# Low halves of the token mix's weights: from a VectorE subtraction to an accumulating transfer

## The chip, the cores and the metric

The kernel runs on one core of one Trainium2 chip. The metric is the device time of one execution in microseconds (us), shown as a median over several runs. Beside it stands one profiled execution with its own time; its trace is where every duration below comes from.

The core has five engines with instruction queues of their own, each worked off in order. PE (TensorE) multiplies matrices; DVE (VectorE), ACT (ScalarE) and POOL (GpSimd) work element by element; SP (SyncE) issues transfers here. Engines wait for one another by semaphores. Transfers (DMA) are carried out by 16 DMA engines that all queues share.

## The reference, cut to what matters

One layer of a decoder with 512 prompt tokens and 64 sample tokens (576 columns), width 1024. A SwiGLU feed-forward stage, then the token mix, then a second feed-forward stage.

```python
z = h @ w_in                                   # 1024 x 10240
u, v, q, k, rv, rg, ga, gb = split(z)
o_a = gelu(u) * chunk_spatial_mix(layer_norm(gelu(v)), gm_ws, gm_bs)
o_r, S_new = retention(rotary(q), rotary(k), rv, S0)        # 8 heads
o_b = head_rms(o_r) * silu(rg)
merged = sigmoid(ga) * (o_a @ w_a) + sigmoid(gb) * (o_b @ w_b)
x = x + g2 * (merged @ w_o)
```

All is float32. The kernel gets its accuracy by splitting each operand into a high part (rounded to the format fp32r) and a low part (the rest, also fp32r), and adds three products: high by high, high by low and low by high.

## The kernel before, in words

Activations lie with features on the 128 partitions and the 576 tokens along the row. A weight matrix is taken in pieces of 128 x 1024 elements (512 KB): eight row blocks of 128 columns, or four blocks of 256, or two of 512.

A piece of the token mix goes through three steps. `load_raw` issues its transfer from HBM on SP's queue into a buffer `wraw`; in the token mix there are three of these. `split_w` takes a buffer `whl` (five here), which holds the high part `hi` and the low part `lo` side by side; ACT writes `hi` by a copy that rounds (line 141), and DVE writes `lo = raw - hi` (line 142). Then PE multiplies with both parts. The `wraw` buffer can be loaded again when `lo` is done, and the `whl` buffer can be written again when PE has done its last product with the piece.

`split_w` is called through `load_w` for 100 pieces, all of the token mix, in this order of program: for each of eight heads the query, key and gate columns (`project`, four pieces; head 0 has its own earlier copies), the value columns (two pieces, PE line 1236) and the head's part of `w_b` (`out_b`, two pieces); then the values of the spatial mix in two halves of four pieces (`values`, PE line 1452, where one bank of results runs over all four pieces); then `gate_u`, `gate_b`, the columns of `ga` and `w_a`, eight pieces each. Most products are of PE line 522. The feed-forward stages and `w_o` split their weights in other functions.

The order of instructions on each engine comes from the framework's scheduler, which plans with its own estimates when the program is built. On the chip it is fixed; an instruction waits until its semaphores are there, and all that stands behind it on its engine waits too. So a change of one instruction moves others on several engines. The prediction speaks of: POOL's rotary additions (line 1189) and copies of the key (1296, 1299); ACT's copy of the decayed key `kd` (1292) for PE's line 1328; the layer norm's gain and bias loads on SP (1520, 1521) and its DVE passes (1525, 1528); POOL's product of mix and gate (1574); ACT's copy (271) for the transposes of the conditioning projection on PE (277), which runs in small steps between the others.

Of the kernel before, what the change touches and what calls it, by code (L numbers as in the profile page):

```python
# [8 lines left out]
F32 = mybir.dt.float32  # L9
F32R = mybir.dt.float32r  # L10
AF = mybir.ActivationFunctionType
ALU = mybir.AluOpType
# [63 lines left out]
def layer_kernel(ctx: ExitStack, tc: tile.TileContext, a):  # L76
    nc = tc.nc
    PE, DVE, ACT, POOL = nc.tensor, nc.vector, nc.scalar, nc.gpsimd
# [56 lines left out]
    def high_low(shape):  # L135
        t = whl([2] + shape)
        return t[:, 0], t[:, 1]

    def split_w(raw, eng=None):
        hi, lo = high_low(list(raw.shape[1:]))  # L140
        ACT.copy(out=hi, in_=raw)  # L141
        (eng or DVE).tensor_tensor(out=lo, in0=raw, in1=hi.bitcast(F32), op=ALU.subtract)  # L142
        return hi, lo

    def load_w(src, k0, kc, c0, cols, eng=None):
        return split_w(load_raw(src, k0, kc, c0, cols), eng)
# [840 lines left out]
    for i in range(2):  # L987
        for n in range(NT):
            m = P if n < 4 else NS
            ACT.activation(  # L990
                out=junk[0:m, i], in_=xtok[n, i], func=AF.Square, accum_out=ss[0:m, i, n:n + 1]
# [54 lines left out]
    for c in range(KC):  # L1046
# [5 lines left out]
        out=t5, in0=r5, scalar=-0.5 / D, in1=r5, op0=ALU.mult, op1=ALU.mult)  # L1052
    steps["r51"] = lambda: DVE.scalar_tensor_tensor(
        out=t5, in0=s5, scalar=D * EPS, in1=t5, op0=ALU.add, op1=ALU.mult)
# [3 lines left out]
        out=xall[:, :, NP:T], in_=psS[:, 0:KC * NS].rearrange("p (c t) -> p c t", c=KC))  # L1058
# [432 lines left out]
    for n in range(NT):  # L1491
# [8 lines left out]
        out=rs.bitcast(I32), in0=t5.bitcast(I32), scalar1=-1.0, scalar2=float(0x5F3759DF), op0=ALU.mult, op1=ALU.add  # L1500
# [7 lines left out]
    for g in range(8):  # L1508
        DVE.tensor_tensor(
            out=wd8[:, g, :].rearrange("p (b l) -> p b l", l=LS),  # L1510
            in0=ws8[:, g, :].unsqueeze(1).broadcast_to([NS, NB, LS]),
            in1=gmc[0:NS, P:P + NS].rearrange("p (b l) -> p b l", l=LS), op=ALU.mult,
# [324 lines left out]
```

## Time and profile before

| | |
|---|---|
| median of 3 runs | 1720.19 us (1717.99 to 1720.61) |
| profiled execution, its own time | 1718.67 us |
| its span (first to last instruction) | 1716.6 us |
| granted TensorE clock, mean | 0.996 |
| PE busy | 1683.7 us (98% of the span) |
| DVE, ACT, POOL busy | 1049.4, 686.6, 209.0 us |
| transfers | 199.5 MB; 38.4% of the 16 engines' time |
| line 141 (ACT), line 142 (DVE) | 100 times each, from 481 to 1225 us |

In the rows of a timeline, the first number is the start in us from the span's start, the second the length; then engine, line, operation, the tile written and those read, and the count of merged instructions. In square brackets stand the idle time of that engine just ahead and what ended it. The names are those of the program without their buffer numbers. A row of stretches gives, for each engine, the busy time in the stretch and the number of instructions, then the granted clock, the mean busy share of the 16 DMA engines and their rate. A row of a group gives the busy time, the mean length of one in ns, and the idle time just ahead of the group with what ended most of it. "PEld" is the loading of weights into PE; "SPq" is SP's queue.

### The profile page before, as it was taken

The page shows a single profiled execution, that of the slowest core. Times are in us where ns is not written, and L with a number is a line of the kernel's source. Part 1 is how long each engine was busy: PE and PEld are TensorE (multiplying, and loading weights), DVE is VectorE, ACT ScalarE, POOL GpSimd, SP SyncE. Part 2 cuts the span into 40 slices and gives each one's busy share as a digit, 9 for nine tenths or more (in the row PEclk, how much of TensorE's full clock was granted, in tenths as well). Part 3 has the DMA queues.
Part 4 walks back from the last instruction along what each step waited for, and adds up shares of the span by engine and source line. Part 5 has one row for each costly group of instructions (what it writes and reads, how often), then busy time and mean ns, then how long its engine had stood idle before and what let it go on. Part 6 is the DMA issues. An engine that isn't in the chain of part 4 may idle for free.

```text
span 1716.6 us, 30444 instructions
## 1 busy us (share of the span) xinstructions
PE 1683.7 (98%) x12588; PEld 1610.9 (94%) x12588; DVE 1049.4 (61%) x1758; ACT 686.6 (40%) x1137; POOL 209.0 (12%) x263
## 2 busy tenths in 40 slices
PE   7999999999999999999999999999999999999997
PEld 4879999999999999999999889999999999999997
DVE  6856847676765745745745546422547958666773
ACT  5533524335534333333333333322235525344354
POOL 0000000000421302302202101220021000000002
PEclk9999999999999999999999999999999999999999
DMA  9443444323454433444424335342330323323231
GB/s 301 132 145 98 134 139 129 99 87 95 146 163 140 142 115 125 132 123 125 149 83 143 100 115 161 103 154 75 99 103 21 87 80 92 99 84 89 86 99 56
DMA packets 279773, 199.52 MB, mean 116 GB/s; under 512 B 9801, under 2 KB 253769, under 8 KB 279634
## 3 DMA queue, kind: packets, MB, share of 16 engines
q1 hardware_dynamic: 279634, 197.58, 38.4%
q8 instruction: 98, 1.61, 0.4%
q14 instruction: 41, 0.34, 0.1%
HBM read 183.12 MB, written 14.42 MB: 115 GB/s over the span
## 4 chain that ended last, share of the span: by engine, by line
PE 88%; DVE 4%; DMA 4%; ACT 2%; issue 1%; SPq 0%; POOL 0%; POOLq 0%; DVEq 0%; ACTq 0%
PE ps L522 47%; PE ps L679 24%; PE ps L1236 5%; PE ps L1452 3%; PE ps L265 2%; DMA wraw<-in_w_down_dram 1%; DMA ada<-in_w_ada_dram 1%; DVE whl L707 1%; PE ps L1366 1%; PE ps L1244 1%; PE ps L1328 1%; DMA xa<-in_w_ada_dram 1%; ACT whl L697 1%; PE ps L1372 1%; PE ps L1344 0%
## 5 line engine op out<-in xcount | busy, mean ns | idle before, releaser
L522 PE MATMUL ps<-xa,whl 128*128 128x288 f32 x2784 | 378.4, 295 | 0.5 <-DVE whl L142 0.3
L522 PEld LDWEIGHTS ps<-xa,whl 128*128 128x128 f32 x2784 | 370.9, 188 | 7.6 <-issue 3.4
L679 PE MATMUL ps<-xa,whl 128*128 128x288 f32 x2064 | 292.8, 296 | 1.9 <-ACT whl L697 1.0
L679 PEld LDWEIGHTS ps<-xa,whl 128*128 128x128 f32 x2064 | 279.1, 188 | 10.5 <-issue 2.5
L142 DVE TENSOR_TENSOR whl<-wraw,whl 128x1024 fp32r<-128x1024 f32 x100 | 126.2, 1270 | 212.4 <-ACT whl L141 208.4
L522 PE MATMUL ps<-c,wd 128*128 128x288 f32 x1824 | 246.7, 295 | 0.0
L522 PEld LDWEIGHTS ps<-c,wd 128*128 128x128 f32 x1824 | 243.2, 188 | 2.6 <-issue 1.7
L679 PE MATMUL ps<-xs,whl 128*128 128x288 f32 x1680 | 239.7, 296 | 1.6 <-ACT sn L688 1.4
L679 PEld LDWEIGHTS ps<-xs,whl 128*128 128x128 f32 x1680 | 228.5, 188 | 7.5 <-ACT sn L688 4.9
L522 PE MATMUL ps<-c,whl 128*128 128x288 f32 x1368 | 194.9, 298 | 0.0
L522 PEld LDWEIGHTS ps<-c,whl 128*128 128x128 f32 x1368 | 184.1, 188 | 2.7 <-DVE S L1391 0.8
L141 ACT CAST whl<-wraw 128x1024 fp32r<-128x1024 f32 x100 | 104.0, 1046 | 107.3 <-PE ps L522 47.6
L509 POOL TENSOR_TENSOR x<-x,s 128x64 f32<-128x64 f32 x72 | 34.4, 478 | 909.4 <-DVE s L508 909.2
L503 DVE SCALAR_TENSOR_TENSOR x<-ps,gate,x 128x288 f32<-128x288 f32 (+1 forms) x128 | 61.5, 483 | 135.3 <-PE ps L522 134.9
L697 ACT CAST whl<-sum 128x1024 fp32r<-128x1024 f32 x80 | 84.0, 1050 | 86.3 <-DVE sum L832 58.2
L707 DVE TENSOR_TENSOR whl<-sum,whl 128x1024 fp32r<-128x1024 f32 x80 | 98.0, 1225 | 30.2 <-ACT whl L697 28.2
L697 ACT CAST whl<-wraw 128x1024 fp32r<-128x1024 f32 (+1 forms) x84 | 70.6, 841 | 98.5 <-PE ps L679 84.8
L1236 PEld LDWEIGHTS ps<-whl,xa 128*128 128x128 f32 x768 | 94.1, 194 | 5.1 <-DVE whl L142 3.4
L1236 PE MATMUL ps<-whl,xa 128*128 128x256 f32 x768 | 95.6, 286 | 3.2 <-DVE whl L142 3.2
L909 ACT CAST wd<-wraw 128x640 fp32r<-128x640 f32 (+2 forms) x58 | 45.3, 782 | 123.6 <-PE ps L522 116.7
L707 DVE TENSOR_TENSOR whl<-wraw,whl 128x1024 fp32r<-128x1024 f32 (+1 forms) x84 | 81.2, 967 | 9.5 <-ACT whl L697 9.1
L688 ACT COPY sn<-ps 128x288 f32<-128x288 f32 x126 | 50.1, 398 | 59.2 <-PE ps L679 57.7
(264 smaller groups left out, 1835.2 us busy)
## 6 DMA issues: line engine op xcount, KB each, us to landing
wraw<-in_w_in_dram SPq DMA_DIRECT2D x80, 512.0 KB
ada<-in_w_ada_dram SPq DMA_DIRECT2D x56, 512.0 KB
wraw<-in_w_gate_dram SPq DMA_DIRECT2D x88, 256.0 KB
wraw<-in_w_up_dram SPq DMA_DIRECT2D x88, 256.0 KB
wraw<-in_w_down_dram SPq DMA_DIRECT2D x32, 384.0 KB
wraw<-in_w_down_dram SPq DMA_DIRECT2D x32, 320.0 KB
S<-in_state_ret_dram SPq DMA_DIRECT2D x32, 256.0 KB
wraw<-in_w_b_dram SPq DMA_DIRECT2D x16, 512.0 KB
```

Of the source, the lines that this page charges most:

```text
L141: ACT.copy(out=hi, in_=raw)
L142: (eng or DVE).tensor_tensor(out=lo, in0=raw, in1=hi.bitcast(F32), op=ALU.subtract)
L503: DVE.scalar_tensor_tensor(out=x[:, o:o + w], in0=ps[:, :w], scalar=g[:, c, 0:1], in1=x[:, o:o + w], op0=ALU.mult, op1=ALU.add)
L509: return lambda: POOL.tensor_tensor(out=x[:, NP:T], in0=x[:, NP:T], in1=u, op=ALU.add)
L522: PE.matmul(ps[:, :H], lhsT=s[:, k, c0:c0 + P], rhs=m[:, HALF[h]], start=k == 0 and z == 0, stop=k == kc - 1 and z == 2,)
L679: PE.matmul(ps[:, :H], lhsT=s[:, j * P:(j + 1) * P], rhs=m[:, j, :], start=fresh and j == 0 and z == 0, stop=j == 3 and z == 2, skip_group ...
L688: ACT.copy(out=t, in_=ps[:, :H])
L697: ACT.copy(out=hl[:, 0], in_=src)
L707: DVE.tensor_tensor(out=hl[:, 1], in0=src, in1=hl[:, 0].bitcast(F32), op=ALU.subtract)
L909: ACT.copy(out=hl[:, 0], in_=self.raw[c])
L1236: PE.matmul(ps[:, :DV], lhsT=s, rhs=m, start=i == 0, stop=i == 23)
L1452: PE.matmul(ps, lhsT=s, rhs=m[:, kx % 2, :], start=kx == 0 and z == 0, stop=kx == KC - 1 and z == len(terms) - 1,)
```

## The change

`split_w` no longer subtracts on DVE. ACT reads the raw weights a second time with scale -1 and writes the rounded negative into `lo`, so that `lo = -hi`; then a transfer issued from POOL's queue reads `raw` and adds it to `lo` in place, in SBUF, so that `lo = raw - hi` as before. PE, the next loads of `wraw`, and everything that waited for DVE's line 142 now wait for the landing of that transfer.

```diff
     def split_w(raw, eng=None):
         hi, lo = high_low(list(raw.shape[1:]))
         ACT.copy(out=hi, in_=raw)
-        (eng or DVE).tensor_tensor(out=lo, in0=raw, in1=hi.bitcast(F32), op=ALU.subtract)
+        ACT.activation(out=lo, in_=raw, func=AF.Copy, scale=-1.0)
+        POOL.dma_start(out=lo, in_=raw, accum_op=ALU.add)
         return hi, lo
```

Lines behind it have numbers one higher in the changed kernel (1189 becomes 1190); line 142 is ACT's negative there, line 143 the transfer.

The scheduler's order changes with it in the token mix. Three places follow on two engines, with buffer numbers in the names (they count up with every tile, so the same tile can have another number).

POOL, first head. Before:

```order
L1189 TENSOR_TENSOR c_5158<-h_5260,h_5261 128x288
L1282 TENSOR_TENSOR qdS<-c_5158,hc_5498 128x8x8
L1189 TENSOR_TENSOR c_5159<-h_5266,h_5267 128x288
L1296 COPY h_5529<-c_5159 128x2x64
L1299 COPY h_5529<-c_5159 128x2x64
L1189 TENSOR_TENSOR c_5463<-h_5492,h_5493 128x288
```

After:

```order
L1190 TENSOR_TENSOR c_5158<-h_5260,h_5261 128x288
L1283 TENSOR_TENSOR qdS<-c_5158,hc_5504 128x8x8
L1190 TENSOR_TENSOR c_5159<-h_5266,h_5267 128x288
L143 DMA whl_5307<-wraw_5305 128x1024
L143 DMA whl_5313<-wraw_5311 128x1024
L143 DMA whl_5447<-wraw_5445 128x1024
L143 DMA whl_5453<-wraw_5451 128x1024
L143 DMA whl_5459<-wraw_5457 128x1024
L143 DMA whl_5465<-wraw_5463 128x1024
L1297 COPY h_5535<-c_5159 128x2x64
L1300 COPY h_5535<-c_5159 128x2x64
```

The transfers of the first six pieces stand behind the last rotary addition of head 0, and the copies of the key stand behind them.

PE, the first value pieces of head 0 (`whl_5307` is the first piece, `whl_5312` before and `whl_5313` after the second). Before:

```order
L1236 MATMUL ps_5318<-whl_5307,xa_4536 128x256 x6
L1236 MATMUL ps_5318<-whl_5307,xa_4537 128x256 x6
L1236 MATMUL ps_5318<-whl_5312,xa_4538 128x256 x6
L1236 MATMUL ps_5318<-whl_5312,xa_4539 128x256 x6
L1236 MATMUL ps_5344<-whl_5307,xa_4536 128x256 x6
```

After:

```order
L1237 MATMUL ps_5320<-whl_5307,xa_4536 128x256 x2
L1237 MATMUL ps_5346<-whl_5307,xa_4536 128x256 x2
L1237 MATMUL ps_5372<-whl_5307,xa_4536 128x256 x2
L1237 MATMUL ps_5398<-whl_5307,xa_4536 128x256 x2
L1245 MATMUL ps_5424<-whl_5307,hs 128x256
L523 MATMUL ps_5473<-xa_4536,whl_5447 128x288 x2
L1267 MATMUL ps_5514<-c_5158,c_5159 128x128
L1237 MATMUL ps_5320<-whl_5307,xa_4536 128x256 x4
L1237 MATMUL ps_5320<-whl_5307,xa_4537 128x256 x6
L1237 MATMUL ps_5320<-whl_5313,xa_4538 128x256 x2
```

The products with the high part alone are drawn ahead for four banks, with four of other kinds behind them; the first that needs the low part comes after these twelve, where it came after two.

PE, second half of `values`. `whl_10910` to `whl_10925` before and `whl_10972` to `whl_10990` after are the same four pieces. Before:

```order
L1452 MATMUL ps_10928<-whl_10910,xa_4536 128x512 x6
L1452 MATMUL ps_10928<-whl_10915,xa_4537 128x512 x6
L1452 MATMUL ps_10928<-whl_10920,xa_4538 128x512 x6
L1452 MATMUL ps_10928<-whl_10925,xa_4539 128x512 x6
L1452 MATMUL ps_10955<-whl_10910,xa_4536 128x512 x6
```

After:

```order
L1453 MATMUL ps_10994<-whl_10972,xa_4536 128x512 x6
L1453 MATMUL ps_10994<-whl_10978,xa_4537 128x512 x2
L1453 MATMUL ps_11021<-whl_10972,xa_4536 128x512 x5
L1453 MATMUL ps_10994<-whl_10978,xa_4537 128x512 x4
L1453 MATMUL ps_10994<-whl_10984,xa_4538 128x512 x2
L1453 MATMUL ps_11021<-whl_10972,xa_4536 128x512
L1453 MATMUL ps_11021<-whl_10978,xa_4537 128x512 x4
L1453 MATMUL ps_10994<-whl_10984,xa_4538 128x512 x4
L1453 MATMUL ps_10994<-whl_10990,xa_4539 128x512 x2
```

The two products of a piece that need only its high part come first, then products of the next bank with the piece that is already there, and only then those that need the low part.

On SP, the loads of the second layer norm's tables stand behind the load of the 81st of the 100 pieces before, which waits for the `wraw` buffer of the 78th, and behind that of the 80th after, which waits for the buffer of the 77th.

## The prediction

> **What bounds the kernel now.** First the page's busy times, then the stretches in which the 100 pieces are split, then PE's waits from 430 to 1260 us.
>
> ```profile
> PE 1683.7 (98%) x12588; PEld 1610.9 (94%) x12588; DVE 1049.4 (61%) x1758; ACT 686.6 (40%) x1137; POOL 209.0 (12%) x263
> 480.00:1230.00 750.00, 745.01 (x5683) 707.76 (x5682) 398.61 (x697) 258.25 (x418) 135.12 (x137) 1.00 0.41 124
> ...
> PE ps L1236 <- DVE whl L142: 3.2, 1, 3.2
> PE ps L277 <- ACT c L271: 1.5, 1, 1.5
> PE ps L402 <- DVE all L391: 0.6, 1, 0.6
> PE ps L522 <- DVE whl L142: 0.3, 1, 0.3
> ```
>
> From 480 to 1230 us PE is busy 745.0 of 750 at full granted clock (columns: PE, PE's loads, DVE, ACT, POOL, clock, DMA share, GB/s). Its waits have four causes worth naming, and the removed subtraction accounts for 3.2 + 0.3 us. DVE is busy 399 of 750 us: it bounds nothing here. A change that unloads DVE can win at most these 5 us; one that makes a low part later than PE needs it loses without a limit. So the question is how late the new low parts come.
>
> **The change, part by part.**
>
> ```profile
> L142 DVE TENSOR_TENSOR whl<-wraw,whl 128x1024 fp32r<-128x1024 f32 x100 | 126.2, 1270 | 212.4 <-ACT whl L141 208.4
> L141 ACT CAST whl<-wraw 128x1024 fp32r<-128x1024 f32 x100 | 104.0, 1046 | 107.3 <-PE ps L522 47.6 <-issue 36.7 <-DMA wraw<-in_w_in_dram 17.4
> q1 hardware_dynamic: 108359, 91.78, 40.2%
> 489.05 0.37 SPq L130 DMA_DIRECT2D wraw<-in_w_in_dram  x1
> 494.45 1.05 ACT L141 CAST whl<-wraw 128x1024 fp32r<-128x1024 f32 x1 [1.58 <-DMA wraw<-in_w_in_dram]
> ```
>
> *Removed:* 100 DVE passes, 126.2 us, worth nothing in themselves. *Added on ACT:* 100 passes like line 141 (1046 ns), 104.6 us; ACT goes from 258 to 363 of 750 us, still not a bound.
>
> *Added on POOL's queue:* 100 transfers of 0.524 MB. No row has an accumulating transfer, nor any issued by POOL. In the 750 us the 16 engines spent 40.2%, 301.5 us, on 91.78 MB (third row), 3.29 us a MB: one plain copy of a piece costs 1.7 us of all engines. An accumulating one reads two operands and writes one. Bounds for its engine time c: 1.7 us (nothing extra) and 5.2 us (each of three streams costs a whole copy). I take 3.4, two copies, because a load reads one operand and this reads two. From issue to landing a load of this size took 494.45 - 489.05 = 5.4 us, 1.7 of it engine time; so I set the landing time L = 3.7 + c: 5.4, 7.1 and 8.9 us. POOL's own issue I count within that; SP's takes 0.37 us, and a POOL pass as long as the longest quoted below, 1.83, would add some 1.5 to each L.
>
> The Trainium skill's page "Collectives: The Full Stack", section on why ReduceScatter is half of AllGather, says that the add itself is free and the second source read halves the rate. By it c would be the same 3.4. No run here shows it.
>
> *For most pieces the delay is hidden.* There are five buffers `whl`, and a piece takes PE 48 products:
>
> ```profile
> 1166.00 94.07 PE ps L522 x710
> SPq L130 <- DVE whl L142: 317.4, 71, 14.0
> ```
>
> At 94.07 / 710 = 0.1325 us each that is 6.4 us a piece. A buffer is filled when PE has finished the piece five before, so four pieces, 25 us, lie between filling and use; 2.1 us on ACT and 7.1 for the landing fit. The second row (SP's queue) says what else hangs on the low part: 71 loads wait for line 142 to free one of three buffers `wraw`. Their cycle becomes 5.4 for the load + 2.1 + 7.1 = 14.6 us, against 19.1 for three pieces of PE's work: it holds, with 4.5 us to spare. The cover is missing where the pipeline starts empty or is emptied; four places.
>
> *A, the first value pieces.*
>
> ```profile
> 483.76 0.40 PE L1236 MATMUL ps<-whl,xa 128*128 128x256 f32 x2
> 486.11 1.83 POOL L1189 TENSOR_TENSOR c<-h,h 128x288 f32<-128x288 f32 x1 [0.24 <-DVE h L1188]
> 487.34 7.41 PE L1236 MATMUL ps<-whl,xa 128*128 128x256 f32 x49 [3.19 <-DVE whl L142]
> ```
>
> The first transfer stands on POOL behind the rotary addition that ends at 487.94, and lands at 487.94 + 7.1 = 495.0; PE resumed at 487.34 before. Since PE's new order draws some ten products ahead of the wait (0.15 us each by the last row), the loss is 7.7 - 1.5 = 6.2. The second piece lands c = 3.4 later, and PE needs it 18 products (2.7 us) later: 0.7 more. A = 6.9 (4.5 at the low bound, 10.5 at the high one).
>
> *B, the first state update (PE line 1328)* needs ACT's `kd` (line 1292), which stands on ACT behind both passes of the seventh piece.
>
> ```profile
> 506.97 0.69 ACT L1292 ACTIVATE c<-ps,hc 128x512 f32<-128x512 f32 x1 [2.94 <-PE ps L1290]
> 507.55 0.47 ACT L1306 ACTIVATE h<-ps,hc 128x256 fp32r<-128x256 f32 x1
> 510.19 1.89 PE L1328 MATMUL ps<-c,c 128*128 128x256 f32 x8
> ```
>
> Pieces 1, 4 and 7 share a `wraw` buffer. From the first landing at 495.0: load of piece 4, 5.4 + 1.7 because two accumulating transfers share the engines; ACT's two passes and a copy between, 2.5; landing, 7.1; load of piece 7, 5.4; ACT's two passes 2.1 and 0.47 + 0.69: `kd` is there at 520.4. PE, shifted by A, wants it at 510.19 + 6.9 = 517.1. B = 3.3 (0.6 and 3.3 at the bounds). The key's copies on POOL, now behind six transfers, come well within this chain.
>
> *C, the second half of `values`,* where three pieces are split in the moment they are needed.
>
> ```profile
> 989.23 2.95 ACT L141 CAST whl<-wraw 128x1024 fp32r<-128x1024 f32 x3 [0.28 <-PE ps L1452]
> 991.83 8.35 PE L1452 MATMUL ps<-whl,xa 128*128 128x512 f32 x36
> 994.44 0.63 ACT L1463 ACTIVATE c<-c 64x512 f32<-64x512 f32 x1 [1.65 <-DVE c L1462]
> ```
>
> The negative is done at 989.23 + 2.1 = 991.3, the low part lands at 998.4. PE now has 13 products that need no late low part (0.232 us each): it wants it at 994.85. That is 3.6; the next two pieces land 3.4 us apart and are wanted after 11 and 10 products, 2.5 and 2.3: 0.9 and 1.1 more. C = 5.6 (2.9 and 10.9).
>
> *D, the second layer norm,* which ends in PE's 1.5 us wait for line 271.
>
> ```profile
> 1059.54 1.04 ACT L141 CAST whl<-wraw 128x1024 fp32r<-128x1024 f32 x1
> 1069.92 0.37 SPq L130 DMA_DIRECT2D wraw<-in_w_in_dram  x1
> 1070.34 0.57 SPq L1520 DMA_DIRECT2D c<-in_gm_ln_g_dram  x1
> 1075.32 1.42 DVE L1525 SCALAR_TENSOR_TENSOR c<-c,mv,c 128x512 f32<-128x512 f32 x2 [2.65 <-DMA c<-in_gm_ln_g_dram]
> 1084.67 0.58 ACT L271 COPY c<-ps 128x512 f32<-128x512 f32 x1 [0.23 <-DVE c L1528]
> ```
>
> The tables load on SP behind a weight load that waits for a `wraw` buffer, now that of the 77th piece (cast at 1059.54) where it was the 78th's. Its landing at 1059.54 + 2.1 + 7.1 = 1068.7, and the tables 0.4 behind, are 1.2 us earlier than 1070.34. I count D as 0 (-1.5 at the low bound).
>
> *E, the DMA engines where loads are densest:*
>
> ```profile
> 560.00:960.00 400.00, 62.69 (x49) 51.27 (x49) 1.00 0.40 125
> 1000.00:1060.00 60.00, 10.88 (x9) 9.71 (x10) 1.00 0.53 147
> ```
>
> (Instructions on `wraw` alone: DVE, ACT, clock, DMA share.) From 1000 to 1060 us the loads take 0.53 x 60 = 31.8 us and ten accumulating transfers 34: 65.8 of 60, 5.8 too many. Elsewhere there is room: 0.40 x 400 + 49 x 3.4 = 327 of 400. E = 5.8 (0 at the low bound).
>
> *Sum:* 6.9 + 3.3 + 5.6 + 0 + 5.8 = 21.6 us on the profiled execution's own 1718.67 us (span 1716.6 and 2.1 around it): 1740.3. The median of the runs lies 1.5 us above that execution, so I say 1741. At the low bound 4.5 + 0.6 + 2.9 - 1.5 = 6.5: 1725. At the high one A to C are 24.7, and over the 750 us the engines would have 0.41 x 750 + 520 = 827.5 us to do, 77.5 too many: 1718.7 + 24.7 + 77.5 = 1821.
>
> **The rivals.** *1, the DMA engines become the bound.* From (750 - 307.5) / 100 = 4.4 us per accumulating transfer on, the token mix runs at their pace, and each further microsecond costs 100. For it: nothing in the trace shows that an add goes at copy speed. Against it: 4.4 is 2.6 copies. At 5.2 the time is 1821; typical 1770 to 1850.
>
> *2, not slower: everything lands in time.* The mechanism is a short landing at place A and C. If L is about 3.2 us, A is 487.94 + 3.2 - 487.34 - 1.5 = 2.3, B is 0, C only 0.7, D gives back 1.5: 1.5 us in all, 1720. It decides from L below about 3.6. For it: nothing but the two bare places is uncovered. Against it: the only row with this size took 5.4.
> The Trainium skill's "DMA: Bandwidth & Descriptors", section on the anatomy of one DMA, gives for a plain transfer issued by GpSimd about 2.0 us and the bytes at 436 GB/s, an estimate of 3.2 us here. By it the time would be 1720; the load above contradicts it with 5.4, though other loads ran beside it.
>
> *3, faster.* The 5 us of idle PE vanish because DVE no longer holds up its queue (it stood 208 us waiting for line 141) and the scheduler packs PE better: 1714. Against it: A alone costs 487.94 - 485.7 = 2.2 us plus L, where PE, after its ten products, would stand from 485.7.
>
> **How the numbers follow.** Forecast (latency at the bare places, 1726 to 1765): 0.58. Rival 1: 0.22. Rival 2: 0.14. Rival 3: 0.06. About 0.2%, 3.4 us, can be told from no change. Slower then is 0.58 + 0.22 = 0.80, same 0.14, faster 0.06. The range runs from 1719, where rival 2 begins to end, to 1830, just above the high bound; it leaves out rival 3, a little of rival 2, and c above 5.2.
>
> **What would show it.** PE waits of 4 to 10 us at the first value product and of 3 to 5 us at the second half of `values`, both ended by a transfer of `whl`; one at line 1329 ended by ACT; none worth naming in 560 to 960 us, where the DMA share should be near 0.8. Line 143 stands 100 times on POOL; DVE loses 126 us and ACT gains 105. A DMA share near 1 with PE waits in every head would be rival 1. The forecast is wrong in its core if most of the lost time lies between 560 and 960 us.

## The result, and the profile after

The changed kernel takes 1745.2 us (median of 4 runs, 1741.8 to 1746.5) against 1720.4 us (median of 4 runs beside it): the ratio is 1.0143, with a 95% interval of 1.0125 to 1.0161. The forecast was 1741 us, slower. The sum behind it was right by compensation: the terms A, B and C came near only together with a slow clock that was not counted at all, E was far too large, and D was missing.

The page of the changed kernel: busy time of the engines, the two ACT passes, the transfer on POOL, the software queue's share of the 16 DMA engines, and the landing time of its transfers.

```profile
PE 1692.8 (97%) x12588; PEld 1615.6 (93%) x12588; DVE 931.7 (54%) x1658; ACT 778.5 (45%) x1237; POOL 275.0 (16%) x363
L142 ACT ACTIVATE whl<-wraw 128x1024 fp32r<-128x1024 f32 x100 | 105.7, 1057 | 0.0
L143 POOL DMA_DIRECT2D whl<-wraw x100 | 86.6, 875 | 465.5 <-ACT whl L142 415.1
q0 software_dynamic: 14400, 52.44, 16.4%
whl<-wraw POOLq DMA_DIRECT2D x100, 512.0 KB, 5.4
```

The change did what it says: 100 negatives on ACT, 100 transfers from POOL, DVE 118 us less. One accumulating transfer costs 16.4% of 1739.6 us / 100 = 2.85 us of all engines and lands a median 5.4 us after its issue. PE's busy time, which the change doesn't touch, went from 1683.7 to 1692.8 us: 9.1 of the 23.0 us by which the span grew are PE working slower, not PE waiting.

PE's waits from 430 to 1300 us (waiting line, releaser; total us, times, longest):

```profile
PE ps L278 <- ACT c L272: 6.9, 1, 6.9
PE ps L1237 <- DMA whl<-wraw: 5.0, 1, 5.0
PE ps L1329 <- ACT c L1293: 3.5, 1, 3.5
PE ps L1453 <- DMA whl<-wraw: 3.3, 3, 1.7
PE ps L523 <- DMA whl<-wraw: 1.0, 1, 1.0
PE ps L523 <- ACT whl L141: 0.8, 1, 0.8
```

Three of the first four are the forecast's places A (line 1237), B (1329) and C (1453). The longest is D (278), which it had counted at zero. At A the last rotary addition, the first transfers and PE's first product with a low part follow one another like this:

```profile
485.30 0.79 POOL L1190 TENSOR_TENSOR c<-h,h 128x288 f32<-128x288 f32 x1 [0.23 <-DVE h L1189]
486.04 2.78 POOL L143 DMA_DIRECT2D whl<-wraw  x3
490.84 1.44 PE L1237 MATMUL ps<-whl,xa 128*128 128x256 f32 x5 [5.01 <-DMA whl<-wraw]
```

Between 560 and 960 us no wait stands, although the DMA share is high (columns as in the stretches shown before):

```profile
560.00:960.00 400.00, 399.67 (x3198) 382.57 (x3198) 179.70 (x374) 189.04 (x285) 115.41 (x137) 1.00 0.75 190
1060.00:1100.00 40.00, 39.09 (x291) 36.30 (x289) 7.14 (x13) 18.95 (x26) 9.64 (x10) 1.00 1.00 235
```

Where the 23.0 us lie shows best when each trace is cut where PE ends its last product with the same weight piece (same work on both sides of a cut). "Slower" is what PE's busy time grew by between the cuts.

| kernel before, us | longer by | PE idle | PE slower |
|---|---|---|---|
| 0 to 483.9, no split piece used | -1.2 | -2.5 | +1.2 |
| 483.9 to 532.0 (A, B) | +10.8 | +6.4 | +4.4 |
| 532.0 to 964.7 (heads) | +0.8 | +0.3 | +0.5 |
| 964.7 to 1025.6 (C) | +4.2 | +3.3 | +0.9 |
| 1025.6 to 1083.8 | +0.7 | +0.7 | 0.0 |
| 1083.8 to 1131.4 (D) | +7.2 | +5.4 | +1.8 |
| 1131.4 to the end | +0.5 | +0.2 | +0.3 |

The first row differs from profile to profile (-1.2 to +3.6 us among the kernels below, where no instruction of that stretch was meant to differ), and it was at its lowest in this profile. The profiled execution of the changed kernel was also the fastest of its four; the medians lie 24.8 us apart, the profiles 23.0.

**PE slower** is for the most part the granted clock behind a wait at A, B and D, 6.2 of the 9.1 us. Stretches of 4 us of the changed kernel, behind A's wait (ended at 490.84) and B's (ended at 516.82); the last three numbers are the clock, the DMA share and GB/s:

```profile
488.00:492.00 4.00, 1.16 (x5) 1.16 (x6) 0.00 (x0) 0.00 (x0) 0.82 (x1) 0.58 1.05 197
492.00:496.00 4.00, 4.00 (x23) 4.00 (x22) 0.00 (x0) 0.00 (x0) 0.00 (x0) 0.56 1.04 155
496.00:500.00 4.00, 4.00 (x36) 4.00 (x35) 0.00 (x0) 0.00 (x0) 0.00 (x0) 1.00 1.09 273
516.00:520.00 4.00, 3.18 (x8) 2.55 (x9) 3.68 (x4) 2.50 (x5) 3.87 (x5) 0.50 0.79 144
520.00:524.00 4.00, 4.00 (x22) 3.91 (x21) 3.80 (x7) 0.78 (x1) 1.79 (x4) 0.65 0.93 286
524.00:528.00 4.00, 4.00 (x57) 3.55 (x55) 2.24 (x6) 0.48 (x2) 1.94 (x4) 1.00 0.78 166
```

After a wait of 5.0 or 3.5 us the clock is near half for some 4 to 6 us, and PE does 23 products in the 4 us from 492 us where it does 36 in those from 496 us. At C, whose three waits are 1.7 us and less, it stays at 1.00 here. C's 0.9 us of slower PE are therefore not the clock: 48 products that took 11.07 us in one run in the kernel before stand in four groups between the waits, which take 3.14 + 2.79 + 2.60 + 3.47 = 12.00 us. In the kernel before, A's wait of 3.2 us had the same tail, shorter:

```profile
488.00:492.00 4.00, 4.00 (x27) 4.00 (x27) 2.25 (x2) 0.45 (x2) 2.40 (x2) 0.72 0.72 199
492.00:496.00 4.00, 4.00 (x35) 4.00 (x35) 1.70 (x2) 2.19 (x3) 0.00 (x0) 1.00 0.84 236
```

The Trainium skill's page "TensorE: Matmul & The Clock Gate", part 1, says that PE's clock is halved after an idle window of about 3.4 us, that the window runs freely, and that full speed returns after a busy one. The traces agree on the window: cut at the right places, every stretch of 3.41 us has a clock of 1.00 or 0.50 and nothing between (0.72 above is a mean over a change). They don't agree that the window must be idle throughout. In the 13 traces of this case the clock fell 25 times between 430 and 1300 us; 24 times PE had been busy for 1.65 us or less of the 3.41 us just before, and once for 2.14. It stayed up behind one stretch with 1.62 us busy, and otherwise only behind stretches with 1.70 us and more. So it is not the length of a wait alone that counts, but how much of one such stretch it takes: a wait of 3.1 us (experiment 8) and the 3.2 us above were followed by half speed, one of 3.4 us (experiment 2) was not. C's three waits (1.2, 0.4 and 1.7 us, some 3 us apart), without a trace in the clock here, were followed by 0.73 for 4 us in experiment 2.

### The profile page after: what moved, and what is told of

Same layout as the page of the kernel before. It is cut to its first block, busy times and chain, and to the rows that moved or that the text cites. A ratio compares the mean times of both kernels' runs of the same rounds, so it can differ in the third digit from the quotient of the medians.

```text
span 1739.6 us, 30724 instructions
## 1 busy us (share of the span) xinstructions
PE 1692.8 (97%) x12588; PEld 1615.6 (93%) x12588; DVE 931.7 (54%) x1658; ACT 778.5 (45%) x1237; POOL 275.0 (16%) x363
## 3 DMA queue, kind: packets, MB, share of 16 engines
q0 software_dynamic: 14400, 52.44, 16.4%
## 4 chain that ended last, share of the span: by engine, by line
PE 58%; DMA 4%; DVE 3%; ACT 1%; issue 1%; SPq 0%; POOL 0%; POOLq 0%; ACTq 0%; DVEq 0%
PE ps L523 34%; PE ps L680 11%; PE ps L1237 4%; PE ps L1453 2%; DMA whl<-wraw 2%; DMA wraw<-in_w_in_dram 1%; DVE whl L708 1%; DMA wraw<-in_w_down_dram 1%; PE ps L1367 1%; PE ps L266 1%; PE ps L1245 1%; PE ps L1329 1%; ACT whl L698 1%; PE ps L1373 1%; PE ps L1345 0%
## 5 line engine op out<-in xcount | busy, mean ns | idle before, releaser
L143 POOL DMA_DIRECT2D whl<-wraw x100 | 86.6, 875 | 465.5 <-ACT whl L142 415.1
L1422 DVE TENSOR_TENSOR c<-c,ps 128x288 f32<-128x288 f32 x112 | 47.2, 450 | 174.4 <-PE ps L523 174.1
L142 ACT ACTIVATE whl<-wraw 128x1024 fp32r<-128x1024 f32 x100 | 105.7, 1057 | 0.0
```

What stands on the lines that cost most here:

```text
L142: ACT.activation(out=lo, in_=raw, func=AF.Copy, scale=-1.0)
L143: POOL.dma_start(out=lo, in_=raw, accum_op=ALU.add)
L1422: DVE.tensor_tensor(out=dst, in0=dst, in1=ps[:, :H], op=ALU.add)
```

## The experiments

The theory after the result: the loss lies at four places alone (A, B and C by the transfer's landing, D by the order on SP's queue together with the slow ring of `wraw` buffers, the three that are loaded in turn) and in the clock behind their waits; the other pieces' transfers cost nothing. The rivals: the transfers cost something everywhere (full DMA engines), or ACT's second pass costs it. Pieces are numbered 0 to 99 in the order in which the program asks for them; "by subtraction" means line 142 of the kernel before. In kernels that choose by piece, line numbers are 4 higher than in the changed kernel (1241 for 1237). Medians stand beside runs of the kernel before on the same chip (1719.5 to 1720.5 us). The last three columns give the stretches of the table above, longer than the kernel before by us.

| kernel | median us | ratio (95% interval) | 484-532 | 965-1026 | 1026-1131 |
|---|---|---|---|---|---|
| changed | 1745.2 | 1.0143 (1.0125 to 1.0161) | +10.8 | +4.2 | +7.9 |
| 1 transfers for pieces 10 to 57 only | 1721.8 | 1.0007 (0.9998 to 1.0015) | +0.9 | 0.0 | -0.6 |
| 2 A and B by subtraction | 1733.1 | 1.0072 (1.0059 to 1.0086) | -0.7 | +5.9 | +6.6 |
| 3 three pieces of B by subtraction | 1741.5 | 1.0122 (1.0107 to 1.0138) | +5.5 | +5.5 | +9.0 |
| 4 pieces 66 to 79 by subtraction | 1733.9 | 1.0081 (1.0067 to 1.0095) | +11.7 | +4.3 | -0.6 |
| 5 tables loaded early | 1733.5 | 1.0079 (1.0065 to 1.0093) | +9.5 | +4.2 | -1.1 |
| 6 A, B, C by subtraction, tables early | 1721.2 | 1.0008 (0.9999 to 1.0017) | +0.7 | 0.0 | -1.0 |
| 7 plain copies, no addition | 1722.1 | 1.0013 (1.0005 to 1.0022) | +3.3 | +1.0 | -2.3 |
| 8 negative on ACT, addition on DVE | 1730.5 | 1.0055 (1.0040 to 1.0069) | +1.4 | +0.2 | +9.0 |
| 9 the same for pieces 66 to 79 only | 1745.9 | 1.0153 (1.0140 to 1.0167) | +9.2 | +4.1 | +10.3 |
| 10 kernel before, two moves | 1719.7 | 0.9999 (0.9990 to 1.0007) | +2.5 | 0.0 | -1.7 |
| 11 kernel before, tables early | 1719.3 | 0.9999 (0.9990 to 1.0009) | +1.5 | 0.0 | -1.7 |

**1. Transfers only where the cover is.**

```diff
+        turn["piece"] += 1
+        if not 10 <= turn["piece"] < 58:
+            DVE.tensor_tensor(out=lo, in0=raw, in1=hi.bitcast(F32), op=ALU.subtract)
+        else:
             ACT.activation(out=lo, in_=raw, func=AF.Copy, scale=-1.0)
             POOL.dma_start(out=lo, in_=raw, accum_op=ALU.add)
```

> Transfers for the 48 pieces numbered 10 to 57 (the last ones of head 1's round to the end of the heads), DVE's subtraction for the other 52. Theory (covered pieces cost nothing): 1719 to 1722 us, with the DMA share between 600 and 950 us near 0.75 as in the changed kernel. Rival (each transfer costs something by contention, wherever it lies): 48 of 100 pieces, about half of the 25 us, 1732 us.

1721.8 us, and in this profile the heads lost 0.6 us (0.5 of it at their beginning), with a DMA share of 0.74 from 565 to 960 us. 48 transfers with five `whl` buffers' lead cost nothing that can be told. The rival of a cost per transfer (some 12 us here) falls.

**2. A and B by subtraction** (the condition above is `turn["piece"] < 8`).

> The changed kernel with DVE's subtraction for the first eight pieces (the first two value pieces, and all up to the second head's value pieces). Theory: from 480 to 535 us it is as before (a wait of some 3.2 us at the first value product, none at the first state update, granted clock 0.98 there), which gives back the 10.7 us that lie between 484 and 532 us in the changed kernel, and leaves what comes later: 1734 us (1731 to 1737). Of the 10.7 only 6.4 are idle time of PE; the other 4.3 are PE at a clock of 0.72 and 0.66 behind the two waits. Rival 1 (the clock drops for another reason, the engines' load for one): the clock stays near 0.7 around 490 to 525 us and 1738 to 1740 us remain. Rival 2 (the delay is only put off: the ring of load buffers starves later): 1741 or more.

1733.1 us. PE's waits in it (430 to 1300 us), and the stretch behind the wait at A:

```profile
PE ps L282 <- ACT c L276: 5.1, 1, 5.1
PE ps L1241 <- DVE whl L144: 3.4, 1, 3.4
PE ps L1457 <- DMA whl<-wraw: 3.4, 3, 1.8
```

```profile
488.00:492.00 4.00, 3.96 (x33) 3.75 (x32) 2.56 (x2) 0.95 (x2) 2.65 (x3) 1.00 0.65 181
492.00:496.00 4.00, 4.00 (x36) 4.00 (x35) 1.22 (x1) 1.47 (x3) 0.00 (x0) 1.00 0.95 275
```

The wait at A is DVE's again, B is gone, the clock is 1.00 with DMA shares of 0.65 and 0.95: the low clock came with the waits, not with the load on the engines. The same trace in stretches of 3.41 us, two at A and two at C:

```profile
482.53:485.94 3.41, 1.70 (x13) 1.49 (x12) 3.27 (x9) 1.91 (x3) 2.19 (x4) 1.00 0.23 81
485.94:489.35 3.41, 1.70 (x12) 1.50 (x12) 3.38 (x4) 0.00 (x0) 3.11 (x3) 1.00 0.14 39
1001.36:1004.77 3.41, 1.64 (x8) 1.04 (x7) 0.00 (x0) 1.78 (x2) 0.85 (x1) 1.00 0.84 240
1004.77:1008.18 3.41, 3.41 (x10) 2.64 (x9) 0.00 (x0) 0.60 (x1) 0.00 (x0) 0.50 0.89 206
```

A's wait of 3.4 us falls half into each of two stretches and leaves PE 1.70 us busy in both, and the clock stays. C's waits leave PE 1.64 us of one stretch, and the next runs at 0.50. C and D stay; what they lose together went from 12.1 to 12.5 us. Nothing was put off to a later place.

**3. B alone.** (`if 3 <= turn["piece"] < 6`.) B's chain in the changed kernel, in order of time:

```profile
500.55 1.05 ACT L141 CAST whl<-wraw 128x1024 fp32r<-128x1024 f32 x1 [14.57 <-DMA wraw<-in_w_in_dram]
503.12 0.85 POOL L143 DMA_DIRECT2D whl<-wraw  x1 [14.29 <-ACT whl L142]
508.16 3.06 SPq L130 DMA_DIRECT2D wraw<-in_w_in_dram  x2
513.83 1.04 ACT L141 CAST whl<-wraw 128x1024 fp32r<-128x1024 f32 x1 [5.63 <-DMA wraw<-in_w_in_dram]
516.09 0.68 ACT L1293 ACTIVATE c<-ps,hc 128x512 f32<-128x512 f32 x1
```

The piece numbered 3 is cast at 500.55, its low part lands at 508.1 and only then is the next load of that `wraw` buffer issued; `kd` follows at 516.09, and PE waits until 516.82.

> The changed kernel with DVE's subtraction for the three pieces numbered 3 to 5 alone (head 1's second to fourth piece); the first two value pieces stay transfers. Theory (place B hangs on the ring of load buffers: the piece numbered 6 can be loaded only when the low part of the piece numbered 3 is there, and ACT's kd stands behind it): the low part of that piece is there some 5 us earlier, the 3.5 us wait at the first state update goes, and with it 2 to 3 us of half clock behind it; the 5.0 us wait at the first value product stays: 1739 us (1738 to 1741). Rival (kd is late because of ACT's passes and the loads' own slowness with full engines, not the transfer): 2 to 3 us of wait stay, 1743 us or more.

1741.5 us; in its place PE's first state update runs without a wait (`kd` done at 515.2, PE there at 518.24), and the stretch gives back 5.3 us of 10.8. PE's longest waits that remain:

```profile
PE ps L282 <- ACT c L276: 7.2, 1, 7.2
PE ps L1241 <- DMA whl<-wraw: 5.0, 1, 5.0
PE ps L1457 <- DMA whl<-wraw: 3.3, 2, 1.9
```

B is the ring, as the forecast said. The edit also takes three of ACT's passes away, but they are not the cause: ACT stood idle for 5.63 us ahead of the cast at 513.83, waiting for the load, and experiment 8, which keeps all of ACT's passes and has no transfer, has no wait at the first state update. The median is half a microsecond above the theory's range: C lost 1.3 us more to a low clock behind waits of the same 3.3 us in all, and D 1.0 us more.

**4. The stretch of D by subtraction** (`66 <= turn["piece"] < 80`).

> The changed kernel with DVE's subtraction for the 14 pieces numbered 66 to 79 (the last w_b pieces, the gate u and the first gate b columns). Theory (the second layer norm's tables come late because the load ahead of them on SP waits for a load buffer, whose low part lands late in a stretch with the DMA engines full): the wait of 6.9 us at line 278 goes back to about 1.5 and the 1.0 us wait before it goes: 1737 us (1735 to 1740). Rival (the tables are late since everything is 15 us later there, by the order on SP alone): 6 to 7 us of waiting stay, 1744 us.

1733.9 us, below the 1735 to 1740 that were expected: the 7.9 us lost from 1026 to 1131 us are gone and 0.6 more. This takes away the transfers there, ACT's second pass and the order that came with both; experiment 5 keeps the first two.

**5. All transfers, but the tables of the second layer norm loaded early.** In the changed kernel the SP queue, the transfers and DVE stand at D like this:

```profile
1082.80 0.88 POOL L143 DMA_DIRECT2D whl<-wraw  x1 [5.07 <-ACT whl L142]
1090.00 1.14 SPq L1521 DMA_DIRECT2D c<-in_gm_ln_g_dram  x1
1095.14 1.42 DVE L1526 SCALAR_TENSOR_TENSOR c<-c,mv,c 128x512 f32<-128x512 f32 x2 [6.81 <-DMA c<-in_gm_ln_g_dram]
```

The transfer issued at 1082.80 lands at 1089.5; the weight load ahead of the tables waited for it, and went out at 1089.6. The tables follow at 1090.00, DVE starts at 1095.14, and PE resumes at 1105.99 after 6.9 us. In the kernel before the tables went out at 1070.34; PE being 15 us later, 1085.6 would have been as early.

```diff
-    second = layer_norm(1, 2.5)
+    second = layer_norm(1, *tables(1), 2.5)
```

(`tables` holds the two loads that stood at the beginning of `layer_norm`; they are issued right behind those of the first layer norm, ten weight loads and one pair of conditioning loads earlier, and not six as the expectation has it.)

> All 100 pieces by transfer, as in the changed kernel; the gain and bias tables of the second layer norm are loaded right behind those of the first, ahead of the six weight loads that stand before them otherwise. Theory (place D: the tables are late because their load stands on SP behind weight loads that wait for a load buffer): the wait of 6.9 us at line 278 falls to 1 us or none, and with it the slow clock behind it: 7 us less, 1738 us (1736 to 1740). Rival (the DMA engines are full from 1060 to 1100 us and everything that ends there is late, the layer norm's own chain with it): the wait stays at 4 us or more, or PE waits for a piece in its place, 1742 us or more.

1733.5 us, below the expected range too: the stretch gave back 9.0 of the 11.7 us between the medians, places A and B 1.3, and the rest shows in no single place. The wait at line 278 is gone, while the engines stay full; 1060 to 1100 us of this kernel:

```profile
1060.00:1100.00 40.00, 40.00 (x299) 37.44 (x298) 12.03 (x21) 20.00 (x28) 11.31 (x12) 1.00 1.04 229
```

PE is busy 40.0 of 40 us beside a DMA share of 1.04. So D was not full engines by themselves, but one small load standing in an in-order queue behind a load that waited for a buffer.

**6. The four places mended, 88 transfers left.**

> The four places mended, the other 88 transfers left as they are: DVE's subtraction for the pieces numbered 0 to 7 and 62 to 65, and the second layer norm's tables loaded behind the first's. Theory (the loss lies at these four places and nowhere else): 10.8, 4.2 and 8.9 us come back, 0.5 to 1 us stays at one more wait on a transfer: 1719 to 1722 us, with the DMA share still 0.75 to 1.0. Rival (what is mended at one place turns up at a later one): 1726 us or more.

1721.2 us, not to be told from the kernel before. Two stretches of it, and its waits:

```profile
565.00:960.00 395.00, 395.00 (x3188) 377.84 (x3187) 176.26 (x371) 185.48 (x281) 111.68 (x134) 1.00 0.76 191
1030.00:1060.00 30.00, 30.00 (x228) 29.00 (x227) 22.24 (x59) 15.18 (x20) 5.18 (x6) 1.00 1.01 231
```

```profile
PE ps L1241 <- DVE whl L144: 3.6, 1, 3.6
PE ps L527 <- DMA whl<-wraw: 1.0, 1, 1.0
```

88 transfers, engines full for 30 us at a time, and only the wait that the kernel before has as well is left, beside 1.0 us. The loss lay at the four places.

**7. What the addition costs.**

```diff
         ACT.activation(out=lo, in_=raw, func=AF.Copy, scale=-1.0)
-        POOL.dma_start(out=lo, in_=raw, accum_op=ALU.add)
+        POOL.dma_start(out=lo, in_=raw.bitcast(F32R))
```

> The transfer on POOL's queue copies the raw piece over the negative instead of adding to it (so the low part is the raw weight, and the products with it mean nothing; work, order and sizes are otherwise the changed kernel's). It prices the addition. Theory, as the prediction counted it (an addition reads a second operand and costs two copies): the software queue's share falls from 16.4% (2.85 us a piece) to about 8.5% (1.5 us), landing falls from 5.4 to about 4 us, the stretch 1060 to 1100 us is no longer full, and the loss is 12 to 16 us of the 25: 1732 us. Rival (the addition goes at copy speed and 2.85 us is what any transfer from one buffer to another costs): share 15 to 16%, 1743 to 1746 us.

1722.1 us. The page of this kernel: the software queue, the transfer on POOL, its landing; and the first of PE's waits.

```profile
q0 software_dynamic: 14400, 52.44, 8.7%
L143 POOL DMA_DIRECT2D whl<-wraw x100 | 55.6, 556 | 468.2 <-ACT whl L142 422.3
whl<-wraw POOLq DMA_DIRECT2D x100, 512.0 KB, 3.8
```

```profile
PE ps L1237 <- DMA whl<-wraw: 3.4, 1, 3.4
```

8.7% of 1721.4 us / 100 = 1.50 us a piece against 2.85: an addition costs 1.9 copies of engine time, 1.6 us more until landing, and 0.3 us more of POOL's issue. The rule of the forecast held (two copies), and the same rule on the Trainium skill's page "Collectives: The Full Stack" (why ReduceScatter is half of AllGather) agrees with these rows. The loss shrank to 2.1 us in the medians, far below the 12 to 16 us that were expected to remain: with the landing 1.6 us sooner and about half the engine time nearly all of it goes, D too (PE's wait at line 278 is gone without any move of the tables). Which of the two does more was not tried apart.

**8 and 9. ACT's second pass without a transfer,** for all pieces and for the 14 of D.

```diff
         ACT.activation(out=lo, in_=raw, func=AF.Copy, scale=-1.0)
-        POOL.dma_start(out=lo, in_=raw, accum_op=ALU.add)
+        DVE.tensor_tensor(out=lo, in0=raw, in1=lo.bitcast(F32), op=ALU.add)
```

> The low part is made by ACT's negative and then by an addition on DVE; nothing is transferred by POOL. It is the change without its transfer. Theory (the transfer's landing makes the loss): 1720 to 1725 us; at the first value product and at the second half of the values DVE starts one ACT pass, 1.05 us, later, nothing else moves. Rival (ACT's second pass is what delays the high parts and ACT's copies for PE): 1730 us or more, with PE's waits ended by ACT.

> The changed kernel, but for the 14 pieces numbered 66 to 79 the raw piece is added to ACT's negative by DVE and not by a transfer. With DVE's subtraction there (ACT's second pass gone as well) the stretch lost nothing against the kernel before; with the transfer it loses 7 to 8 us. Theory (the transfers alone): 0 to 1 us lost from 1084 to 1131 us, 1734 to 1736 us in all. Rival (half of it is ACT's second pass and the order that comes with it, as the 3.4 us that the kernel with 100 additions on DVE lost there say): 3 to 4 us lost there, 1737 to 1740 us.

Both went against the theory: 1730.5 us where 1720 to 1725 stood, and 1745.9 where 1734 to 1736 did. The rival's mechanism is not what the trace shows either: PE's waits in the first of them, and the place of the longest,

```profile
PE ps L266 <- DMA ada<-in_w_ada_dram: 4.0, 1, 4.0
PE ps L278 <- ACT c L272: 3.3, 1, 3.3
PE ps L1237 <- DVE whl L143: 3.1, 1, 3.1
```

```profile
1038.54 1.07 PE L266 MATMUL ps<-ada,cs 128*32 128x512 f32 x8
1039.63 7.56 SPq L302 DMA_DIRECT2D ada<-in_w_ada_dram  x4
1043.58 3.21 PE L266 MATMUL ps<-ada,cs 128*32 128x512 f32 x8 [3.97 <-DMA ada<-in_w_ada_dram]
```

Two groups of the conditioning projection stand one behind the other on PE (in the kernel before, their first instructions are 40 us apart, at 1039.34 and 1079.36); the second needs the loads that the first makes room for, so PE waits 4.0 us for them, and the weight loads stand behind these four loads on SP until 1047.3. The tables are then issued at 1083.64, some 3 us late for PE, and line 278 waits 3.3 us. Elsewhere the 100 additional ACT passes cost little: +1.4 and +0.2 in the table, and -0.2 us from 532 to 965 us. So the loss goes with a new order on PE and SP, which the scheduler drew up for the other durations. That it is the order alone, and not in part the ring with one pass more, was not tried apart. Since the order moves with any edit in this stretch, run 4 cannot be read as the price of the transfers there; runs 5 and 7, in which PE never waits at line 266, can.

**10 and 11. The kernel before, mended.** Run 11 loads the tables early; run 10 also writes the first two value pieces' loads ahead of the first head's rotary products.

```diff
+        wv = [load_w(win, 4 * i, 4, RV0 + hd * DV, DV) for i in range(2)] if hd == 0 else None
```

> The kernel before, with DVE's subtraction for all pieces, and two moves: the second layer norm's tables loaded behind the first's, and the first two value pieces' loads and splits written ahead of the first head's rotary products (the order then has their subtraction one pass earlier on DVE). Theory (what is left to gain is the idle time of PE at the two places and the slow clock behind them): 1.5 us at the layer norm, 0.5 to 3 at the first value product: 1716 to 1718 us. Rival (the moves shift the order elsewhere and cost as much): 1719 to 1722 us.

> The kernel before with the second layer norm's tables loaded behind the first's, and nothing else. Theory: the 1.5 us wait at line 277 and 0.2 us of slow clock go, nothing else moves: 1718.3 us, 0.1% less, at the edge of what can be told. Rival: no difference.

1719.7 and 1719.3 us. In both profiles the wait at line 277 is gone and that stretch is 1.7 us shorter, but the wait at A was 4.3 and 3.6 us (3.2 before) with 1.4 and 1.1 us of low clock more, and the medians can't be told from the kernel before. No version beat it.

## Why the prediction was right, step by step

- **The bound.** Right. PE had 5 us to win and DVE's relief won nothing: DVE fell by 118 us of 1049, the span grew.
- **c, the engine time of an addition: 3.4.** Measured 2.85. "Two copies" was right; a copy costs 1.50 us, not 1.7.
- **L, issue to landing: 7.1 = 3.7 + c.** Measured a median of 5.4, 4.5 at the least and 4.8 for the first at A (486.04 to 490.84). The mis-sized term is the 3.7, which was taken from a load out of HBM beside other loads; 4.5 - 2.85 leaves 1.7, and the plain copy's least, 2.8, less 1.5 leaves 1.3. That copy landed in 3.2 us at A (issued at 489.21, PE resumed at 492.38): just the estimate that the Trainium skill's "DMA: Bandwidth & Descriptors", anatomy of one DMA, gave for a plain transfer, which the prediction put aside on the strength of that load. Rival 2 (not slower, from L below about 3.6) is what the kernel without addition does, at 1722 us.
- **A, 6.9.** Right mechanism: PE waited for the first transfer 5.0 us, where it had waited 3.2 for DVE. Besides the landing, the start was late in the sum: the last rotary addition took 0.79 us and not 1.83, so the transfer went out 3.5 us behind PE's first product and not 4.2. With B mended the stretch lost 5.5 us, of it 2.3 by the low clock.
- **B, 3.3.** Right, ring and all: 3.5 us of wait ended by ACT. With the clock behind it 5.3 us.
- **C, 5.6.** Right, three waits of 1.2, 0.4 and 1.7 us and 0.9 us more for the broken run of products: 4.2. The bounds of this term don't follow from its working: at the low bound it gives 991.3 + 5.4 - 994.85 = 1.9 and not 2.9, and with rival 2's landing nothing and not 0.7.
- **D, 0.** Wrong, and the largest wait. The step that failed is "cast at 1059.54 + 2.1 + 7.1": it took the 77th piece's cast from the trace of before, as if the ring arrived there at its old pace. It was cast at 1080.49, 20.9 us later where PE was 15.3 later: the ring had fallen behind by 5.6 us.
- **E, 5.8.** Only 0.7 us as waits for a piece. The engines filled up later and less than computed (a share of 0.81 from 1000 to 1060 us where 65.8 of 60 us had been put down, 1.00 from 1060 to 1100), and PE hardly felt it directly, with five `whl` buffers; it came out as D, through the tables on SP. D and E together were 5.8, measured 7.9, and the early tables gave it all back.
- **Not counted: the clock.** Most of the 6.2 us by which PE was slower at A, B and D, of 23.0 in all. The row of before that would have told it (0.72 behind A's wait of 3.2 us) was in the trace.
- **The sum.** 21.6 forecast; measured 5.5 + 5.3 + 4.2 + 7.9 = 22.9 at the places and 0.1 elsewhere (+0.8 in the heads, +0.5 at the end, -1.2 at the start). That the two agree is luck: as idle time of PE, which is what the terms stood for, A to C were 9.7 us against 15.8, and landing times too long by 1.7 to 2.3 us made up for the clock. (1740.3 and 1.5 are 1742, not 1741.)
- **What was to show it.** As stated: waits of 5.0 and 3.3 us ended by transfers, one at line 1329 ended by ACT, none in the heads at a DMA share of 0.75. ACT's busy time rose by 92 us and not 105, since a pass begins 0.1 us before the one ahead ends; DVE's fell by 118 and not 126.

## What to carry to other kernels

Price a longer latency where the pipeline starts empty, and then ask of every queue that is served in order what stands behind the thing that has become late: here a small table load behind a weight load cost more than any late weight. Add to a wait of PE of about 3 us or more the products that may follow it at half clock, 1 to 3 us for each here. And when an experiment changes durations in a kernel whose order a scheduler draws up, look at the order first: two of these runs seem to have measured another order and not the operation.

## What the runs showed of the hardware

- An accumulating transfer within SBUF took 1.9 times the engine time of a plain copy (2.85 and 1.50 us for 0.524 MB), landed 1.6 us later (medians 5.4 and 3.8) and held POOL 0.86 us instead of 0.53 at its issue.
- PE's granted clock was halved for 3.4 to 10.2 us at a time, in whole steps of 3.41 us. In 24 of 25 cases PE had been busy for at most 1.65 us of the step before; a wait of 3.4 us that lay half in each of two steps (1.70 us busy in both) left the clock at 1.00, one of 3.1 us did not.
- Three waits of 1.2, 0.4 and 1.7 us, about 3 us apart, left the clock at 1.00 in one profile and were followed by 0.73 (mean of 4 us) in another.
- Full DMA engines (shares of 1.00 to 1.04 over 30 to 40 us) slowed PE by nothing as long as no waiting instruction stood in front of something needed.
